# A hybrid attention and linear-attention layer: a gate's bank emptied ahead of the keys' low parts, and one gate half in another bank

## The chip, the core and the metric

The kernel runs on one core of a Trainium2 chip. The metric is the device time of one execution in microseconds, and the time before is the median of three runs. TensorE multiplies matrices into eight PSUM banks; VectorE (DVE) and ScalarE (ACT) read those banks and work on SBUF; GpSimd (POOL) does small jobs on SBUF; transfers are issued from SyncE's queue (SP) for the most part. Each engine takes its instructions in the order in which they stand in its own list and stops at one whose inputs or buffer aren't ready.

## The reference, cut to what matters

One encoder layer on 1024 tokens (a grid of 16 rows of 64) with 16 meta tokens in front, `D_MODEL` = 1024. After an RMS norm one projection gives all parts; eight pairs of heads do neighbourhood attention on the grid, four heads do gated linear attention in both directions. Both are gated with SiLU, joined, projected back and added to the input.

```
z = rmsnorm(h) @ w_in
gq, gk, gv, r_f, r_b, g_gate, nq, nk, nv, n_gate = split(z)
# neighbourhood attention, 16 heads of 64
qn, kn = rmsnorm(nq), rmsnorm(nk)
o_na = softmax(qn kn^T * scale + bias over an 8 x 16 window and 16 meta keys) @ nv * silu(n_gate)
# gated linear attention, 4 heads, both directions, chunked
o_gla = rmsnorm(scan(q, k, v, decay_f) + reversed scan(q, k, v, decay_b)) * silu(g_gate)
out = h + concat(o_gla, o_na) @ w_out
```

Everything is float32 to the caller. The kernel splits each operand of a large product into a high part and a low part (what the high part leaves out), and makes the product from three matmuls: high x high, high x low, low x high.

## The kernel before, in words

**A filler and a main line.** TensorE's list is put together when the program is built. The *filler* is a generator of the large projections, in which there is always something to multiply; the *main line* is the attention of the eight pairs (`attn_all`), and after it the four scans (`gla`). The class `Sched` keeps an estimated TensorE clock, `S.pe`. The main line yields `("gap", ns)` to let the filler issue that much estimated work, `("to", x)` to let it run up to a point, and `("need", key)` to let it run until `key` is in `S.done`. Work that should come some time later is put off with `S.defer(ns, fn)`. So numbers such as `PK_NS`, `TAIL_NS` and `ATTN_NS` set where an instruction stands, on every engine at once; they aren't waits on the chip.

**The projections.** For each pair `p` the filler issues `dense_na(p)`, eight tiles `pn_na` (b = 0 to 7) of queries, keys and values with 8 x 3 matmuls each, and then `dense_gate(p)`, the pair's gate, transposed, in two halves of 512 tokens (`pz_na`, 8 x 3 matmuls each; the second half lags by four steps). These tiles take turns in two PSUM banks, tag `pd`. A bank is free again when VectorE or ScalarE has read it. A gate's half is read by `gate_evac` (L480), one VectorE instruction that multiplies it by the tokens' norm factors and writes it to `ng`. After the last pair come the scans' projections in the same two banks: queries and keys (`gz`, tiles `pz_gz`), values (`gv`), and the scans' gates (`gg`, tiles `pz_gg`, `dense_gg`): two sets of 128 columns, each in two halves of 512 tokens. In the trace's names all four are `pz_gg`, and their evacuations write `gt`.

**The turn of a pair.** When `dense_na(p)` is done, `k_prep(p)` transposes the keys (`kt`) and meta keys (`kmt`) and `q_prep` the first queries (`qt`), while the filler is in the second half of that pair's gate. ScalarE makes the high parts of the keys, `K1` (L667), VectorE the queries' low parts (L699, L701), the meta keys (L670, L671) and then, in four instructions of 64 x 512, the keys' low parts, `K2` (L676). In the trace both K1 and K2 are named `K`. The first scores (`s`, L725 with K1 and L726 with K2) follow some matmuls later. L807 multiplies the previous pair's output, in bank `po`, by its gate.

**A scan.** `gla(h)` first makes the decays (`pdec`, then VectorE's and ScalarE's work on `ga` and `gm`), then goes backward through eight chunks (`state`: a transpose `pk`, its high and low part `kn`, and the three matmuls of `pu`), then forward (`pa`, masked to `at`, in parts `ah`; outputs `po`, which take the bank `po` and a `ps` bank in turn; `post` norms, transposes, `po00t` and so on, and multiplies by the gate, `og`). The gap `PK_NS[h]` stands between the decays and the first transpose `pk`. The filler issues the next projections beside it; weight pieces are split on ScalarE (`wh`, L260) and VectorE (`wl`, L261) as soon as an earlier piece's slot is free.

Of the kernel before, what the change touches and what calls it, by code (L numbers as in the profile page):

```python
# [20 lines left out]
NPAIR = 8  # L21
# [12 lines left out]
ATTN_NS = 7000.0  # L34
NORM_NS = (1500.0, 2100.0)
VLOAD_NS = (1514.0, 651.0)
TAIL_NS = (2000.0, 700.0, 800.0)
PV_AT = (0.5, 0.5, 0.5, 0.6, 0.5, 0.5, 0.5, 0.5)
STEP_AT = (0.78, 2.0, 3.0, 4.0, 4.92, 6.0, 7.08, 8.0)
BWD_NS = (1800.0, 1523.0, 1844.0, 1892.0)  # L40
PK_NS = (2300.0, 2300.0, 2300.0, 2300.0)
AT_NS = 1085.0
R_NS = 2800.0
R0_NS = 1200.0
# [13 lines left out]
LAG = 4  # L58
# [83 lines left out]
def kernel(  # L142
# [28 lines left out]
    S = Sched()  # L171
    ctx.enter_context(tc.manual_schedule())

    def f32(ap):
        return ap.bitcast(F32)
# [13 lines left out]
    def ps_tile(tag, name, bufs):  # L189
        return psum.tile([128, 512], F32, tag=tag, name=name, bufs=bufs)  # L190

    def pt_tile(name, hold):

        S.pt_free = S.pe + hold
        return ps_tile("pt", name, 1)

    def pt_wait():
        if S.pt_free > S.pe:
            yield ("gap", S.pt_free - S.pe)
# [75 lines left out]
    def pump():  # L275
        assert nsplit[0] < allowed[0] or nsplit[0] >= len(pieces)
        piece_split(nsplit[0])
        nsplit[0] += 1

    def release(ns=0.0):  # L280

        allowed[0] += 1
        S.defer(ns, lambda: pump() if nsplit[0] < allowed[0] else None, late=True)
# [17 lines left out]
    def zt_tile(name, pool_=None):  # L301
        if pool_ is not None:
            return pool_.tile([128, 1024], F32, tag="zt2", name=name, bufs=2)
        return shr.tile([128, 1024], F32, tag="zt", name=name, bufs=3)
# [102 lines left out]
    def mm3(ps, ah, al, bh, bl, start, stop):  # L407
        pe.matmul(ps, ah, bh, start=start, stop=False)  # L408
        pe.matmul(ps, ah, bl, start=False, stop=False)  # L409
        pe.matmul(ps, al, bh, start=False, stop=stop)  # L410
# [28 lines left out]
            yield 3 * (c1 - c0) / 2.4  # L439
        return ps  # L440

    def transposed(key, c0, evac, pump_last=False, lag=LAG):

        ps = [None, None]
        ws = slice(c0, c0 + 128)
        order = sorted([(k + lag * half, half, k) for half in range(2) for k in range(NKB)])
        for _, half, k in order:
            if k == 0:
                ps[half] = ps_tile("pd", f"pz_{key[0]}{key[1]}_{c0}_{half}", 2)
            while (key, k) not in split:  # L450
                pump()
            wh, wl, last = split[(key, k)]
            ts = slice(half * 512, half * 512 + 512)
            mm3(ps[half], wh[:, ws], wl[:, ws], uh[:, k, ts], ul[:, k, ts], k == 0, k == NKB - 1)
            if pump_last and half == 1 and last:
                release()
            if k == NKB - 1:
                evac(ps[half], half)
            yield 648
# [16 lines left out]
    def gate_evac(ps, dst, half):  # L476
        hs = slice(512 * half, 512 * half + 512)
        d = seq_view(dst)[:, 4 * half : 4 * half + 4]
        src, r = (t.rearrange("p (b r c) -> p b r c", b=4, r=16, c=8) for t in (ps, rbc[:, hs]))
        dve.tensor_tensor(d, src, r, OP.mult)  # L480
# [148 lines left out]
    def dense_gate(p):  # L629
        g = zt_tile(f"ng{p}")  # L630
        zt[("ng", p)] = g
        yield from transposed(("na", p + 1), 0, lambda ps, half: gate_evac(ps, g, half), pump_last=p == 7)
        silu.append((p, g))
        yield 0


# [2 lines left out]
    def v_load(p):  # L639

        moves = [(VM, vnat[p]), (VM[7::8], vm_scr[p][:, None, :].to_broadcast([16, 8, 128]))]
        return [S.defer(VLOAD_NS[0] + VLOAD_NS[1] * t, lambda m=m: sp.dma_start(*m)) for t, m in enumerate(moves)]

    def k_prep(p):

        kv = kvm[p]
        yield from pt_wait()
        pm = pt_tile(f"kmt{p}", KMT_NS)
        pe.transpose(pm[:, 0:16], kv[:, 0:128], ident[:16, :16])
        dve.tensor_scalar(kmr, pm[:, 0:16], gk_t, None, OP.mult)  # L650
        srcs = []
        for hb in range(2):
            pt = ps_tile("pp", f"kt{p}_{hb}", 2)
            for bb in range(4):
                pe.transpose(pt[:, bb * 128 : bb * 128 + 128], nat[p][4 * hb + bb][:, 128:256], ident)
            srcs.append(pt.rearrange("p (b t) -> p b t", b=4))
        yield ("w", 970)
        yield from pt_wait()
        q_prep(p, 0)
        yield ("w", 220)  # L660
        km = kmr[:, None, :].to_broadcast([128, 8, 16])
        rows = (slice(0, 64), slice(64, 128))
        for hb in range(2):
            bs = slice(4 * hb, 4 * hb + 4)
            for a in range(2):
                r = rows[a]
                act.activation(K1[a][r, bs, 0:128], srcs[hb][r], AF.Copy, scale=gk_t[r])  # L667
        for a in range(2):
            r = rows[a]
            dve.tensor_copy(K1[a][r, :, 128:BLK], km[r])  # L670
            dve.tensor_tensor(K2[a][r, :, 128:BLK], km[r], f32(K1[a][r, :, 128:BLK]), OP.subtract)  # L671
        for hb in range(2):
            bs = slice(4 * hb, 4 * hb + 4)
            for a in range(2):
                r, o = rows[a], rows[1 - a]
                dve.scalar_tensor_tensor(  # L676
                    K2[a][r, bs, 0:128], srcs[hb][r], gk_t[r], f32(K1[a][r, bs, 0:128]), OP.mult, OP.subtract
                )
                pool.tensor_scalar(K1[a][o, bs], f32(K1[a][r, bs]), 1.0, 0.0, OP.mult, OP.add)
# [53 lines left out]
    po = {}  # L733
# [77 lines left out]
    def attn_all():  # L811


        wait, done = [], []

        def turn():
            p, u, *rest = wait.pop(0)
            done.append((p, u, transposes(p, u, *rest)))

        def gather():  # L820
            while done:
                pv(*done.pop(0))

        for p in range(NPAIR + 1):
            if p < NPAIR:
                yield ("need", ("nat", p))
            if wait:
                turn()
                yield ("w", 654)
                yield ("gap", TAIL_NS[0])  # L830
                turn()
                yield ("w", 654)
                yield ("gap", TAIL_NS[1])
            if p < NPAIR:
                yield from k_prep(p)
            if done:
                yield ("gap", TAIL_NS[2])
                gather()
                yield ("w", 1420)
            if p == NPAIR:  # L840
                break
            vload = v_load(p)
            if p in WD_AT:
                wd_load(WD_AT.index(p))
                S.defer(WD_NS, lambda d=WD_AT.index(p): wd_prep(d))
            if p == NPAIR - 2:
                r_static()
            yield ("gap", ATTN_NS - (TAIL_NS[2] + 1420.0 if p else 0.0))
            f0 = S.fill
            f1 = (p + 1) * (NAT_NS + GATE_NS) + (NAT_NS if p < 7 else GLA_NS - 9000.0)  # L850
            for s in range(8):
                if len(wait) == 2:
                    turn()
                    yield ("w", 654)
                wait.append((p, s, *softmax(p, s)))
                yield ("w", 460 if s in (0, 7) else 700)
                if s == 2:
                    wt_load(2 * p + 2)
                a0 = STEP_AT[s - 1] if s else 0.0
                t0, t1 = (f0 + (f1 - f0) * (a0 + (STEP_AT[s] - a0) * x) / 8 for x in (PV_AT[s], 1.0))  # L860
                yield ("to", t0)
                if s in (0, 2, 4):
                    yield from pt_wait()
                    q_prep(p, s // 2 + 1)
                    yield ("w", 220)
                if s % 2 and s > 1:
                    if s == 3:
                        for m in vload:
                            m()
                    gather()  # L870
                    yield ("w", 1420)
                yield ("to", t1)
            wt_load(2 * p + 3)
# [96 lines left out]
    def dense_gg(h, between=None):  # L970
        key = ("gg", h)
        g = gpool[0].tile([128, 2, 1024], F32, tag="gt", name=f"gt{h}")
        for f in range(2):
            if f == 1 and between is not None:
                between()
            evac = lambda ps, half: gate_evac(ps, g[:, f], half)
            yield from transposed(key, 128 * f, evac, pump_last=f == 1)
        gts[h] = g
        S.done.add(("gg", h))
        yield 0  # L980
# [40 lines left out]
    def gla(h):  # L1021
# [105 lines left out]
        act.activation(ma, mg, AF.Exp, scale=-T16, bias=mt[:, 48:49])  # L1127
        yield ("gap", PK_NS[h])

# [345 lines left out]
```

## Time and profile before

| | |
|---|---|
| median of three runs | 1137.01 us (1136.85 to 1138.11) |
| the profiled execution | 1136.87 us, its span 1134.5 us |
| TensorE busy | 1112.4 us, 98% of the span |
| VectorE, ScalarE, GpSimd busy | 731.1, 549.6, 207.9 us |
| mean granted TensorE clock | 0.998 |
| eight pairs of attention, with their projections | about the first 610 us |
| scans and output projection | the rest |

Rows of the timeline read: start in us from the span's start, duration in us, engine, line, operation, output<-inputs, shape, count, and in brackets the idle time before it with what ended it. `PEld` is TensorE's weight load, which runs ahead of the matmul. Matmuls overlap: their starts, not their durations, give their pace. Rows of the view of waits read: who waited, for whom, and then us in total, number of waits, the longest. `+6 lines` has to be kept in mind for the new kernel: from its line 633 on its lines have higher numbers than the old ones (L676 is L681, L807 is L812, L1155 is L1161).

### The profile page before, as it was taken

The numbers are of one execution on the slowest core, as the hardware profiler recorded it, in microseconds if no ns is written. First come the engines' busy times: TensorE is split into PE (matmuls) and PEld (weight loads), VectorE is DVE, ScalarE is ACT, GpSimd is POOL, SyncE is SP. The second block draws the span as 40 slices with busy tenths as digits, with TensorE's granted clock in tenths as the row PEclk, the third lists the DMA queues.
The fourth block names the chain that finished last, engine by engine and source line by source line (L and its number), as shares of the span: only waits on it lengthen the run. The fifth ranks groups of instructions, "written<-read, shape, count | busy, mean of one in ns | idle before, by whom it ended". The sixth has DMA issues, their size and how long they took to land.

```text
span 1134.5 us, 18937 instructions
## 1 busy us (share of the span) xinstructions
PE 1112.4 (98%) x6739; PEld 982.0 (87%) x6739; DVE 731.1 (64%) x1818; ACT 549.6 (48%) x1436; POOL 207.9 (18%) x430
## 2 busy tenths in 40 slices
PE   8999999999999999999999999999999999999998
PEld 8999898988989889898798789889879978888886
DVE  4666666676666767666664875776586577656352
ACT  6756475664656647465555542642443244313120
POOL 2633232332323223232100001001101100000000
PEclk9999999999999999999999999999999999999999
DMA  8810202112021210301124412513512364414132
GB/s 273 234 53 20 103 10 83 55 39 84 9 83 55 79 52 2 119 12 59 50 66 121 141 47 80 154 26 89 166 38 71 107 208 150 121 43 133 50 114 102
DMA packets 75621, 99.20 MB, mean 87 GB/s; under 512 B 6597, under 2 KB 46917, under 8 KB 75529
## 3 DMA queue, kind: packets, MB, share of 16 engines
q1 hardware_dynamic: 69640, 88.70, 25.1%
q0 software_dynamic: 5600, 9.18, 3.1%
q8 instruction: 53, 0.87, 0.3%
q14 instruction: 40, 0.32, 0.1%
q10 hardware_dynamic: 288, 0.14, 0.0%
HBM read 72.76 MB, written 21.04 MB: 83 GB/s over the span
## 4 chain that ended last, share of the span: by engine, by line
PE 81%; DVE 10%; ACT 4%; issue 1%; DMA 1%; POOL 1%; SPq 0%; ACTq 0%; DVEq 0%; POOLq 0%
PE pn_na L408 6%; PE pn_na L409 6%; PE pn_na L410 6%; PE pout L408 5%; PE pout L410 5%; PE pout L409 5%; PE po L797 3%; PE pp L778 3%; PE pn_gv L408 3%; PE pn_gv L409 3%; PE pn_gv L410 3%; PE pz_gz L408 3%; PE pz_gz L409 2%; PE pz_gz L410 2%; PE pz_na L410 2%; PE pz_na L409 2%
## 5 line engine op out<-in xcount | busy, mean ns | idle before, releaser
L408 PE MATMUL pn_na<-wh,uh 128*128 128x384 f32 x512 | 179.0, 350 | 9.0 <-DVE ng L480 7.1
L409 PE MATMUL pn_na<-wl,uh 128*128 128x384 f32 x512 | 173.2, 338 | 0.2 <-DVE wl L261 0.2
L410 PE MATMUL pn_na<-wh,ul 128*128 128x384 f32 x512 | 172.9, 338 | 0.0
L261 DVE SCALAR_TENSOR_TENSOR wl<-raw,gT,wh 128x256 fp32r<-128x256 f32 (+4 forms) x168 | 89.6, 571 | 38.3 <-ACT wh L260 37.3
L408 PEld LDWEIGHTS pn_na<-wh,uh 128*128 128x128 f32 x512 | 96.6, 189 | 16.6 <-DVE ng L480 9.3
L408 PE MATMUL pout<-wh,oh 128*128 128x512 f32 x256 | 103.2, 403 | 0.2 <-DVE acc L1327 0.2
L260 ACT ACTIVATE wh<-raw,gT 128x256 fp32r<-128x256 f32 (+4 forms) x168 | 87.9, 576 | 28.5 <-PE pz_gz L409 18.0
L410 PE MATMUL pout<-wh,oh 128*128 128x512 f32 x256 | 101.4, 396 | 0.0
L409 PE MATMUL pout<-wl,oh 128*128 128x512 f32 x256 | 101.3, 396 | 0.0
L409 PEld LDWEIGHTS pn_na<-wl,uh 128*128 128x128 f32 x512 | 96.9, 189 | 0.9 <-DVE wl L261 0.5
L410 PEld LDWEIGHTS pn_na<-wh,ul 128*128 128x128 f32 x512 | 96.7, 189 | 0.1
L750 ACT ACTIVATE P<-P,sm 128x384 f32<-128x384 f32 x96 | 58.5, 609 | 78.0 <-DVE sm L745 77.3
L1327 DVE TENSOR_TENSOR acc<-acc,pout 128x512 f32<-128x512 f32 x64 | 43.8, 685 | 66.7 <-PE pout L410 66.7
L213 POOL TENSOR_SCALAR post<-post 128x1 f32<-128x1 f32 x32 | 6.7, 209 | 379.4 <-ACT on L1203 379.4
L214 POOL TENSOR_TENSOR ss<-ss,epsm 128x4 f32<-128x4 f32 x64 | 74.7, 1167 | 5.3
L408 PE MATMUL pn_gv<-wh,uh 128*128 128x256 f32 (+1 forms) x256 | 75.1, 293 | 0.0
L745 DVE CUSTOM_DVE_ANT_0 P<-s,wt 128x416 f32<-128x416 f32 (+1 forms) x128 | 65.4, 547 | 12.6 <-PE s L726 11.7
L409 PE MATMUL pn_gv<-wl,uh 128*128 128x256 f32 (+1 forms) x256 | 72.7, 284 | 0.0
L410 PE MATMUL pn_gv<-wh,ul 128*128 128x256 f32 (+1 forms) x256 | 72.7, 284 | 0.0
L766 DVE TENSOR_SCALAR P<-P,sm 128x384 f32<-128x384 f32 (+1 forms) x128 | 58.3, 455 | 11.5 <-ACT P L750 0.5
L410 PEld LDWEIGHTS pout<-wh,oh 128*128 128x128 f32 x256 | 48.2, 188 | 11.7
L408 PEld LDWEIGHTS pout<-wh,oh 128*128 128x128 f32 x256 | 48.2, 188 | 11.6 <-issue 0.7
(345 smaller groups left out, 2803.8 us busy)
## 6 DMA issues: line engine op xcount, KB each, us to landing
raw<-in_w_na_dram SPq DMA_DIRECT2D x56, 256.0 KB, 3.4
v_scr<-gvst SPq DMA_DIRECT2D x64, 128.0 KB, 2.3
raw<-in_w_o_dram SPq DMA_DIRECT2D x32, 256.0 KB, 3.0
oin<-o_scr SPq DMA_DIRECT2D x32, 256.0 KB, 3.0
v<-v_scr POOLq DMA_DIRECT2D x4, 1536.0 KB, 9.4
VM<-vnat SPq DMA_DIRECT2D x8, 512.0 KB, 3.5
o_scr<-ng SPq DMA_DIRECT2D x8, 512.0 KB, 2.8
raw<-in_w_gz_dram SPq DMA_DIRECT2D x16, 256.0 KB, 2.7
```

Source lines behind the costliest of these rows:

```text
L214: pool.tensor_tensor(dst, dst, epsm[: dst.shape[0], :eng_n], OP.pow)
L260: act.activation(wh[:, ts], r[:, ts], AF.Copy, scale=g)
L261: dve.scalar_tensor_tensor(wl[:, ts], r[:, ts], g, f32(wh[:, ts]), OP.mult, OP.subtract)
L408: pe.matmul(ps, ah, bh, start=start, stop=False)
L409: pe.matmul(ps, ah, bl, start=False, stop=False)
L410: pe.matmul(ps, al, bh, start=False, stop=stop)
L745: dve.tensor_tensor_reduce(P[:, :n], ps[:, :n], wt[2 * p + a][:, off : off + n], -1.0, 3.0e38, OP.add, OP.min, mx)
L750: act.activation(loc, loc, AF.Exp, scale=-1.0, bias=mx, accum_out=sm[:, a : a + 1])
L766: dve.tensor_scalar(loc, loc, r, None, OP.mult)
L778: pe.transpose(pp[:w, c * 128 : c * 128 + 128], Ps[a][0][:, c0 : c0 + w], ident)
L797: pe.matmul(po[0][64 * a : 64 * a + 64, u4 * 128 : u4 * 128 + 128], V[:, 64 * a : 64 * a + 64], PT[a][:w, c * 128 : c * 128 + 128], start= ...
L1327: dve.tensor_tensor(a, a, ps, OP.add)
```

## The change

The diff, whole but for its context lines. `transposed` takes the tag of each half's bank as a parameter.

```
-PK_NS = (2300.0, 2300.0, 2300.0, 2300.0)
+PK_NS = (3500.0, 2300.0, 2300.0, 2300.0)
...
-    def transposed(key, c0, evac, pump_last=False, lag=LAG):
+    def transposed(key, c0, evac, pump_last=False, lag=LAG, tags=(("pd", 2), ("pd", 2))):
...
-                ps[half] = ps_tile("pd", f"pz_{key[0]}{key[1]}_{c0}_{half}", 2)
+                ps[half] = ps_tile(tags[half][0], f"pz_{key[0]}{key[1]}_{c0}_{half}", tags[half][1])
...
         silu.append((p, g))                      # dense_gate
+        S.done.add(("gate", p))
...
+    k_at = [0.0]
...
+        k_at[0] = S.pe                           # k_prep, behind the meta keys, ahead of the K2 loop
+        yield ("need", ("gate", p))
         for hb in range(2):
...
-                yield ("gap", TAIL_NS[2])        # attn_all
+                yield ("gap", TAIL_NS[2] - (S.pe - k_at[0] if p < NPAIR else 0.0))
...
-            yield ("gap", ATTN_NS - (TAIL_NS[2] + 1420.0 if p else 0.0))
+            yield ("gap", ATTN_NS - (TAIL_NS[2] + 1420.0 if p else S.pe - k_at[0]))
...
-            yield from transposed(key, 128 * f, evac, pump_last=f == 1)      # dense_gg
+            tags = (("pd", 2), ("pd", 2) if f else ("po", 1))
+            yield from transposed(key, 128 * f, evac, pump_last=f == 1, tags=tags)
```

There are three parts. At the turn of each pair the program waits, while it is built, until the filler has issued the whole gate, and only then issues the four K2 instructions; the gaps behind it are shortened by what the filler issued meanwhile. In `dense_gg` the second half of the first 128 columns takes the bank `po` in place of a `pd` bank. And in scan 0 the gap ahead of the first `pk` is 3500 in place of 2300 estimated ns.

VectorE at the turn from pair 1 to pair 2, first before, then changed (`ng` from `pz_na_0_1` is the evacuation of the gate's second half, `K_0`, `K_1` with `kt` are the K2 parts of the two heads):

```order
L671 TENSOR_TENSOR K_1_94<-kmr,K_1_92 64x8x16
L676 SCALAR_TENSOR_TENSOR K_0_93<-kt_0_1569,gk_t,K_0_91 64x4x128
L676 SCALAR_TENSOR_TENSOR K_1_94<-kt_0_1569,gk_t,K_1_92 64x4x128
L676 SCALAR_TENSOR_TENSOR K_0_93<-kt_1_1574,gk_t,K_0_91 64x4x128
L676 SCALAR_TENSOR_TENSOR K_1_94<-kt_1_1574,gk_t,K_1_92 64x4x128
L480 TENSOR_TENSOR ng_1478<-pz_na_0_1_1513,rbc 128x4x16x8
L807 TENSOR_TENSOR ng_695<-po_1430,ng_695 128x4x16x8
```

```order
L674 TENSOR_TENSOR K_1_94<-kmr,K_1_92 64x8x16
L480 TENSOR_TENSOR ng_1478<-pz_na_0_1_1513,rbc 128x4x16x8
L681 SCALAR_TENSOR_TENSOR K_0_93<-kt_0_1569,gk_t,K_0_91 64x4x128
L681 SCALAR_TENSOR_TENSOR K_1_94<-kt_0_1569,gk_t,K_1_92 64x4x128
L681 SCALAR_TENSOR_TENSOR K_0_93<-kt_1_1574,gk_t,K_0_91 64x4x128
L681 SCALAR_TENSOR_TENSOR K_1_94<-kt_1_1574,gk_t,K_1_92 64x4x128
L812 TENSOR_TENSOR ng_695<-po_1430,ng_695 128x4x16x8
```

The evacuation moved ahead of the four K2 instructions, at this turn and at the seven others; at the last one a weight split `wl` moved with it. TensorE's, ScalarE's, GpSimd's and SyncE's lists are the same through the whole attention.

VectorE in scan 0 from the second columns' first evacuation on, before and changed (`pk` and `pu` are the backward steps, `hm,gm` the forward decay's scan):

```order
L480 TENSOR_TENSOR gt_7351<-pz_gg_128_0_7502,rbc 128x4x16x8
L261 SCALAR_TENSOR_TENSOR wl_7561<-raw_7397,gT,wh_7560 128x256 x2
L1155 TENSOR_TENSOR kn_7572<-pk_7570,kn_7572 128x128
L261 SCALAR_TENSOR_TENSOR wl_7582<-raw_7411,gT,wh_7581 128x256 x2
L1155 TENSOR_TENSOR kn_7594<-pk_7592,kn_7594 128x128
L1178 TENSOR_SCALAR SB_7569<-pu_7597,c_7479 128x256
L1131 SCALAR_TENSOR_TENSOR mt_7432<-mt_7432,gkm_6654 128x16
L1072 SCALAR_TENSOR_TENSOR ga_7488<-hm,gm_7489 128x1024
L480 TENSOR_TENSOR gt_7351<-pz_gg_128_1_7524,rbc 128x4x16x8
```

```order
L480 TENSOR_TENSOR gt_7351<-pz_gg_128_0_7502,rbc 128x4x16x8
L261 SCALAR_TENSOR_TENSOR wl_7561<-raw_7397,gT,wh_7560 128x256 x2
L261 SCALAR_TENSOR_TENSOR wl_7575<-raw_7411,gT,wh_7574 128x256 x2
L1161 TENSOR_TENSOR kn_7586<-pk_7584,kn_7586 128x128
L480 TENSOR_TENSOR gt_7351<-pz_gg_128_1_7524,rbc 128x4x16x8
L261 SCALAR_TENSOR_TENSOR wl_7597<-raw_7426,gT,wh_7596 128x256 x2
L1161 TENSOR_TENSOR kn_7612<-pk_7610,kn_7612 128x128
L1184 TENSOR_SCALAR SB_7583<-pu_7615,c_7479 128x256
L1137 SCALAR_TENSOR_TENSOR mt_7432<-mt_7432,gkm_6654 128x16
L1078 SCALAR_TENSOR_TENSOR ga_7488<-hm,gm_7489 128x1024
```

The first `kn` now has two pairs of weight splits ahead of it, and the last evacuation of the gates stands ahead of the decay's scan.

VectorE at the first forward step of scan 0, before and changed (`gt` times `gq` and `gk` are the four gate products, `og` the gated output):

```order
L1207 SCALAR_TENSOR_TENSOR on_7810<-po_7775,post_7809,gn 128x256
L614 TENSOR_TENSOR gt_7351<-gt_7351,gq_6516 128x512 x2
L614 TENSOR_TENSOR gt_7351<-gt_7351,gk_6517 128x512 x2
L1217 TENSOR_TENSOR og_7845<-po00t,gt_7351 128x256
L1235 TENSOR_TENSOR at_7851<-pa_7848,tri 128x128
L1236 COPY_PREDICATED at_7851<-tri,pa_7848 128x128
L1238 CAST ah_7854<-at_7851 128x128
```

```order
L1213 SCALAR_TENSOR_TENSOR on_7816<-po_7792,post_7815,gn 128x256
L614 TENSOR_TENSOR gt_7351<-gt_7351,gq_6516 128x512
L261 SCALAR_TENSOR_TENSOR wl_7846<-raw_7455,gT,wh_7845 128x256 x2
L614 TENSOR_TENSOR gt_7351<-gt_7351,gq_6516 128x512
L614 TENSOR_TENSOR gt_7351<-gt_7351,gk_6517 128x512 x2
L1223 TENSOR_TENSOR og_7859<-po00t,gt_7351 128x256
L1241 TENSOR_TENSOR at_7865<-pa_7862,tri 128x128
L1242 COPY_PREDICATED at_7865<-tri,pa_7862 128x128
L1244 CAST ah_7868<-at_7865 128x128
```

A weight split now stands between the first two gate products. In scans 1, 2 and 3 all lists keep their order.

## The prediction, made before the changed kernel ran

> **What bounds the kernel now.** I read the page's busy shares first, then TensorE's waits, the timeline around each wait, and last the windows of stretches without one.
>
> ```profile
> span 1134.5 us, 18937 instructions
> PE 1112.4 (98%) x6739; PEld 982.0 (87%) x6739; DVE 731.1 (64%) x1818; ACT 549.6 (48%) x1436; POOL 207.9 (18%) x430
> ```
>
> TensorE is busy for 98% of the span, so a change is worth what it takes from TensorE's pauses, or adds to them. These are the pauses that the change is about, from the view of waits (in total, how many, the longest; the whole list comes to 18 us):
>
> ```profile
> PE pn_na L408 <- DVE ng L480: 7.1, 7, 1.3
> PE pz_gg L408 <- DVE gt L480: 2.6, 2, 1.5
> ...
> PE pz_gz L408 <- DVE ng L480: 1.6, 1, 1.6
> ```
>
> All ten waits name L480, the evacuation of a gate's bank: seven at the turns to pairs 1 to 7, one at the turn to the scans, two inside the scans' gates. One turn in the timeline:
>
> ```profile
> 195.29 0.40 PE L410 MATMUL pz_na<-uh,wl 128*128 128x512 f32 x1
> ...
> 198.81 3.04 DVE L676 SCALAR_TENSOR_TENSOR K<-kt,gk_t,K 64x512 fp32r<-64x512 f32 x4
> ...
> 201.16 0.34 PE L409 MATMUL pn_na<-wl,uh 128*128 128x384 f32 x1
> ...
> 201.33 0.34 PE L410 MATMUL pn_na<-wh,ul 128*128 128x384 f32 x1
> ...
> 201.89 0.69 DVE L480 TENSOR_TENSOR ng<-pz_na,rbc 128x512 f32<-128x512 f32 x1
> ...
> 202.50 0.68 DVE L807 TENSOR_TENSOR ng<-po,ng 128x512 f32<-128x512 f32 x1
> ...
> 202.63 0.44 PE L408 MATMUL pn_na<-wh,uh 128*128 128x384 f32 x1 [0.96 <-DVE ng L480]
> ...
> 202.91 0.34 PE L409 MATMUL pn_na<-wl,uh 128*128 128x384 f32 x1
> ...
> 204.42 0.29 PE L726 MATMUL s<-K,Q 128*128 128x272 f32 x1
> ```
>
> The gate's second half was complete at 195.69. VectorE could have emptied it at 198.81, but first made the four low parts of the keys (3.04 us); the next projection tile but one, `pn_na` of b=1, needs that bank from 201.50 on and gets it at 202.58. A wait costs more than its idle time: matmuls start 0.17 us apart (201.16, 201.33), the next start came 1.30 later, and the one behind it after 0.28. That is (1.30 - 0.17) + (0.28 - 0.17) = 1.24 for a listed 0.96: idle time plus 0.28, of which I take 0.27 for every wait (the 512-wide ones, 0.235 apart, give 0.26).
>
> **The change, part by part.** *The turns.* The second half's evacuation now stands before the four low parts. Its input has been there since 195.69, so it runs from 198.81 to 199.50, and TensorE asks for the bank at 201.50: 2 us to spare. The other turns have the same rows in the same order (the low parts' x32 are 742 to 758 ns each), so all eight waits go: 7.1 + 1.6 + 8 x 0.27 = **10.9 us**. Bounds: the idle time alone is 8.7; by the weight loads' waits it is 9.3 + 2.1 = 11.4:
>
> ```profile
>   PEld pn_na L408: 9.3, 7
> ...
>   PEld pz_gz L408: 2.1, 1
> ```
>
> What is late next: the low parts end 0.69 later, at 202.54, while TensorE comes 1.24 earlier. Their first reader is the second `s` matmul, L726: 204.42 - 1.24 = 203.18, 0.6 us to spare. At the first turn the wait is longer (1.31 + 0.27 = 1.58); the low parts would end at 62.22 + 3.04 + 0.69 = 65.95, the reader come at 67.84 - 1.58 = 66.26, 0.3 us to spare. The turn to the scans is in the last two fences: its wait is 1.65 + 0.27 = 1.92, and there one weight split (0.51) also goes ahead of the low parts; they end at 545.76 + 0.69 + 0.51 = 546.96 at the latest, the reader comes at 549.53 - 1.92 = 547.61.
>
> ```profile
> 62.22 3.04 DVE L676 SCALAR_TENSOR_TENSOR K<-kt,gk_t,K 64x512 fp32r<-64x512 f32 x4
> ```
>
> ```profile
> 66.05 0.44 PE L408 MATMUL pn_na<-wh,uh 128*128 128x384 f32 x1 [1.31 <-DVE ng L480]
> ...
> 67.84 0.29 PE L726 MATMUL s<-K,Q 128*128 128x272 f32 x1
> ```
>
> ```profile
> 545.76 0.69 DVE L480 TENSOR_TENSOR ng<-pz_na,rbc 128x512 f32<-128x512 f32 x1
> 546.37 0.51 DVE L261 SCALAR_TENSOR_TENSOR wl<-raw,gT,wh 128x288 fp32r<-128x288 f32 x1
> ```
>
> ```profile
> 546.50 0.50 PE L408 MATMUL pz_gz<-uh,wh 128*128 128x512 f32 x1 [1.65 <-DVE ng L480]
> ...
> 549.53 0.28 PE L726 MATMUL s<-K,Q 128*128 128x272 f32 x1
> ```
>
> [...] L807 and the store behind it move by under 0.1 us; TensorE needs neither before the next pair's outputs, some 20 us later. Nothing else moves on any engine before the scans, and the reordered pacing gaps leave TensorE's order as it was, so I cost them at nothing.
>
> *The bank of the scans' gates.* The first columns' second half goes to `po`, so the second columns' second half takes the first half's bank, long empty. Two waits, 2.6 + 2 x 0.27 = **3.1 us** (2.6 to 3.7), go: 1.46 + 0.27 = 1.73 of it in scan 0, the other 1.36 in scan 2. `po` is free then: it is used by the attention's and the scans' outputs alone, and a scan's outputs begin only when its gates are done.
>
> *What takes their place.* Behind both waits VectorE works for some 10 us without a pause, and TensorE now comes to that stretch sooner. Scan 0 as it is:
>
> ```profile
> 632.23 0.50 PE L408 MATMUL pz_gg<-uh,wh 128*128 128x512 f32 x1 [1.46 <-DVE gt L480]
> ...
> 634.40 0.91 ACT L260 ACTIVATE wh<-raw,gT 128x256 fp32r<-128x256 f32 x2 [0.54 <-PE pz_gg L409]
> ...
> 634.94 0.88 DVE L261 SCALAR_TENSOR_TENSOR wl<-raw,gT,wh 128x256 fp32r<-128x256 f32 x2 [1.08 <-ACT wh L260]
> ...
> 637.23 0.27 PE L1152 MATMUL pk<-ident,ga 128*128 128x128 f32 x1
> ...
> 639.40 0.29 DVE L1155 TENSOR_TENSOR kn<-pk,kn 128x128 fp32r<-128x128 f32 x1
> ...
> 639.81 0.32 PE L410 MATMUL pu<-v,kn 128*128 128x256 f32 x1
> ```
>
> VectorE's run starts with the weight split, which can move up by ScalarE's 0.54 alone. The later first transpose (`PK_NS`) lets two groups of three matmuls pass, 2 x 0.70: `pk` comes at 637.23 - 1.73 + 1.40 = 636.90, and the last `pu` matmul, three groups behind it as before, at 639.48. The new order has a second pair of splits (0.80) ahead of `kn`, which so ends at 639.69 - 0.54 + 0.80 = 639.95: **+0.5 us** (0 to 0.8).
>
> A second one is in scan 0's forward part:
>
> ```profile
> 663.66 1.29 DVE L614 TENSOR_TENSOR gt<-gt,gk 128x512 f32<-128x512 f32 x2
> ...
> 664.01 0.38 PE L1215 MATMUL po00t<-ident,on 128*128 128x128 f32 x2
> ...
> 664.86 0.42 DVE L1217 TENSOR_TENSOR og<-po00t,gt 128x256 f32<-128x256 f32 x1
> ...
> 665.85 0.23 DVE L1238 CAST ah<-at 128x128 fp32r<-128x128 f32 x1
> ...
> 666.83 0.40 PE L409 MATMUL pz_gz<-ul,wh 128*128 128x512 f32 x1
> ...
> 667.26 0.91 ACT L260 ACTIVATE wh<-raw,gT 128x256 fp32r<-128x256 f32 x2 [3.98 <-PE pz_gz L409]
> 667.30 0.28 PE L408 MATMUL po<-vx,ah 128*128 128x256 f32 x1
> ```
>
> The matmul `po<-ah` comes 3.29 behind the transpose `po00t`. In the new order a weight split stands after the first of the four gate products, and its slot is freed by the matmul group right in front of `po00t`. With P for that transpose: the slot's L409 starts at P - 0.47, ScalarE's half follows 0.43 later and VectorE's split 0.55 after that, at P + 0.51 to 1.39; three products follow (0.64 each, to 3.2), then `og`, and the cast ends 1.22 behind `og`'s start: P + 4.4, against P + 3.3. **+1.2 us** with the restart (0, if the split waits for nothing; 2.2, the split's 0.88 and a 1.3 us pause in front of it, if none of the present margin of 1.2 is left).
>
> ```profile
> 830.76 0.28 DVE L1155 TENSOR_TENSOR kn<-pk,kn 128x128 fp32r<-128x128 f32 x1
> ...
> 831.84 0.28 PE L410 MATMUL pu<-v,kn 128*128 128x256 f32 x1
> ```
>
> In scan 2 the order is unchanged; VectorE gains about the same 0.54 and TensorE 1.36, and the margin of 831.84 - 831.04 = 0.80 covers the difference of 0.82 but for a trace, there and at the `pu` two steps on: **+0.15** (0 to 0.5).
>
> Sum: -10.9 - 3.1 + 0.5 + 1.2 + 0.15 = -12.1. The profiled execution took 1136.87 us (the span and 2.4 around it), 0.14 under the median of 1137.01; 1136.87 - 12.1 = **1124.8 us**.
>
> **The rivals.** *No new waits* (0.20): the run on VectorE keeps up, and all of 14.0 stays: 1122.9. For it: in the present trace neither `kn` nor `ah` is waited for in scan 0; against it: the two sums above miss by 0.5 and 1.1. *The keys' low parts become the wait* (0.10): if they end 1.0 us later than worked out, `s` waits 0.4 with 0.1 for its restart at seven turns and 0.8 at the first, 4.3 in all: 1129.1. It decides where a margin of 0.6 (0.3 at the first turn) is used up. For it: they are moved back, in front of a reader that comes sooner; against it: no row shows work that would delay them further. *The turns' wait stays* (0.04), because the bank is held by something else than the evacuation's place: then only the scans change, -3.1 + 1.85, 1135.6. Against it: the wait ends 0.05 behind L480's end. *Slower* (0.03): with its pauses gone TensorE is granted a lower clock. The price is in the windows (columns: stretch, length, busy time of five engines, clock, DMA):
>
> ```profile
> 0.00:70.00 70.00, 65.47 (x358) 61.58 (x358) 40.10 (x101) 47.35 (x127) 30.00 (x56) 0.98 0.73 224
> ...
> 825.00:925.00 100.00, 100.00 (x608) 87.93 (x607) 67.27 (x157) 40.25 (x90) 7.55 (x18) 1.00 0.34 98
> ```
>
> With the first stretch's 0.98 in the rest too, 70 + (1124.8 - 70)/0.98 = 1146; below 0.989 the gain is gone. But 100 us without a pause ran at 1.00. [...]
>
> **How the numbers follow.** The forecast has 0.63, with 1123.5 to 1126.5 as its own range. From the clean case with 0.6 below it to the late low parts: 1122.3 to 1128.5. A difference of 0.2% (2.3 us) is about what can be told here: the first three cases are faster (0.93, with a little left for a mishap), the fourth is no change (0.04), the fifth slower (0.03).
>
> **What would show it.** Right: no wait of `pn_na` or `pz_gz` on `ng` L480 in the waits, none of `pz_gg` on `gt`; L480's second half directly behind the casts of the meta keys; new waits of `pu` on `kn` near 639 and of `po` on `ah` near 665 (both earlier by some 10 us), under 2 us together. Wrong: `s` waiting for K, the old waits still there, or a clock below 0.99.

## The result

The changed kernel takes 1124.2 us (median; 1123.46 to 1125.54) against 1136.93 for the kernel before, measured beside it on the same chip: a ratio of 0.9885, 95% interval 0.987 to 0.99. It is faster by 1.15%. The profiled execution took 1124.28 us, where 1124.8 was forecast. Its page (span; busy time and share of the span, by engine):

```profile
span 1122.3 us, 18940 instructions
PE 1109.8 (99%) x6739; PEld 981.6 (87%) x6739; DVE 730.5 (65%) x1818; ACT 549.3 (49%) x1436; POOL 207.8 (19%) x430
```

The mean granted clock was 1.000 (0.998 before). TensorE's largest waits in the changed kernel (us in total, how many, the longest):

```profile
PE po L802 <- DVE PT L789: 2.1, 3, 1.0
PE po L408 <- DVE ah L1244: 1.6, 2, 0.9
PE pn_na L408 <- ACT uh L360: 1.1, 1, 1.1
PE warm L345 <- POOL ones L341: 1.0, 1, 1.0
PE pu L410 <- DVE kn L1161: 0.9, 3, 0.3
PE pn_na L408 <- ACT wh L260: 0.6, 1, 0.6
PE pu L408 <- ACT kn L1160: 0.4, 1, 0.4
```

The three rows that the prediction began with, of `pn_na` and `pz_gz` on `ng` and of `pz_gg` on `gt`, are gone. The largest row now, `po` on `PT`, is no new one: before, as L797, it stood in the same list with 2.2, 3, 1.0. (`PT` is the copy out of PSUM of a transposed piece of the softmax's weights; ScalarE makes it for a pair's first head, VectorE for the second, and the attention's `po`, the product with the values, reads both.) The same turn as in the prediction, VectorE and then TensorE:

```profile
195.38 0.69 DVE L480 TENSOR_TENSOR ng<-pz_na,rbc 128x512 f32<-128x512 f32 x1
195.99 3.07 DVE L681 SCALAR_TENSOR_TENSOR K<-kt,gk_t,K 64x512 fp32r<-64x512 f32 x4
199.09 0.69 DVE L812 TENSOR_TENSOR ng<-po,ng 128x512 f32<-128x512 f32 x1
```

```profile
197.90 0.34 PE L410 MATMUL pn_na<-wh,ul 128*128 128x384 f32 x1
198.07 0.34 PE L408 MATMUL pn_na<-wh,uh 128*128 128x384 f32 x1
198.24 0.34 PE L409 MATMUL pn_na<-wl,uh 128*128 128x384 f32 x1
...
199.63 0.29 PE L730 MATMUL s<-K,Q 128*128 128x272 f32 x1
199.75 0.29 PE L731 MATMUL s<-K,Q 128*128 128x272 f32 x1
199.88 0.29 PE L730 MATMUL s<-K,Q 128*128 128x272 f32 x1
200.00 0.29 PE L731 MATMUL s<-K,Q 128*128 128x272 f32 x1
```

The evacuation ends at 196.07. The matmul that waited before is the one at 198.07 (at 202.63 in the fence of the kernel before), and it now starts 0.17 behind the one in front of it. The low parts end at 199.06.

Where the time went can be read matmul by matmul, since TensorE's list has 6739 matmuls in both kernels and the same order outside scan 0: the n-th start of one trace less the n-th start of the other is the time won up to there. The table is worked out from both traces in that way.

| stretch, in us of the kernel before | forecast | measured |
|---|---|---|
| start-up, to 28 | 0 | -0.67 |
| the eight turns, 28 to 550 | -10.9 | -10.90 |
| scans 0 and 1, 550 to 800 | -1.73 + 0.5 + 1.2 = -0.03 | -0.33 |
| scan 2, 800 to 840 | -1.36 + 0.15 = -1.21 | -1.20 |
| the rest | 0 | +0.72 |
| sum | -12.1 | -12.38 |

The start-up owes nothing to the change: all engines' lists are the same in both kernels up to the first turn, and among the traces of this study TensorE comes to the 60th microsecond up to 1.5 us sooner or later, by the waits of `pn_na` on `uh` and `wh` (the high parts of the inputs and of the weights; 1.9 us on `wh` before, 1.1 on `uh` and 0.6 on `wh` changed). The clock of 0.998 before belongs here as well: it was 0.66 from 12 to 17 us, and 1.00 over the rest of the start-up, from 28 to 550 us and from 550 us on. So the gain behind the start-up is not one of the clock.

### The profile page after: what moved, and what is told of

Its sections match the earlier page's. It is cut to its first block, busy times and chain, and to the rows that moved or that the text cites. A ratio compares the mean times of both kernels' runs of the same rounds, so it can differ in the third digit from the quotient of the medians.

```text
span 1122.3 us, 18940 instructions
## 1 busy us (share of the span) xinstructions
PE 1109.8 (99%) x6739; PEld 981.6 (87%) x6739; DVE 730.5 (65%) x1818; ACT 549.3 (49%) x1436; POOL 207.8 (19%) x430
## 4 chain that ended last, share of the span: by engine, by line
PE 87%; DVE 5%; ACT 3%; DMA 2%; issue 1%; POOL 1%; SPq 0%; DVEq 0%; ACTq 0%; POOLq 0%
PE pn_na L408 7%; PE pn_na L410 6%; PE pn_na L409 6%; PE pout L408 5%; PE pout L410 5%; PE pout L409 5%; PE po L802 4%; PE pp L783 3%; PE pn_gv L408 3%; PE pn_gv L410 3%; PE pn_gv L409 3%; PE pz_na L410 3%; PE pz_na L409 3%; PE pz_na L408 3%; PE pz_gz L408 3%; PE pz_gg L408 3%
## 5 line engine op out<-in xcount | busy, mean ns | idle before, releaser
L408 PEld LDWEIGHTS pout<-wh,oh 128*128 128x128 f32 x256 | 48.2, 188 | 12.1 <-issue 0.7
```

## The experiments

### The turns alone, and the bank alone

The first kernel has the new order at the turns and the scans as before. Against the changed kernel:

```
-PK_NS = (3500.0, 2300.0, 2300.0, 2300.0)
+PK_NS = (2300.0, 2300.0, 2300.0, 2300.0)
...
-            tags = (("pd", 2), ("pd", 2) if f else ("po", 1))
+            tags = (("pd", 2), ("pd", 2))
```

> The turns alone: the evacuation of each gate's second half ahead of the four low parts, the scans as before (both halves of the first columns in pd, first gap 2300). By the theory that each turn's wait is the bank held behind the low parts, all eight waits go and nothing takes their place: 1136.9 - 10.9 = 1126.0 us, with the two waits of pz_gg on gt (2.6 us) still listed. By the rival that the gain came from elsewhere (a clock of 1.00 in place of 0.998, or the start of the program, where a transfer's wait differs from run to run), the turns alone bring less than 7 us: 1130 or more.

Measured: 1126.41 us (1125.73 to 1127.55), ratio 0.9901, 0.9888 to 0.9915. In this trace the waits on `ng` are gone, and the scans' stayed:

```profile
PE pz_gg L408 <- DVE gt L480: 2.6, 2, 1.5
```

The n-th starts differ from the kernel before by -0.84 at 28 us, -11.56 at 550 and -11.54 at 925. So the turns are worth 10.7 us by this trace, and no part of that is given back in the scans. The rival's 1130 or more is out.

The second kernel has `po` for the gates' bank and the old order everywhere else. Against the kernel before (with `transposed` taking tags, as in the change):

```
-            yield from transposed(key, 128 * f, evac, pump_last=f == 1)
+            tags = (("pd", 2), ("pd", 2) if f else ("po", 1))
+            yield from transposed(key, 128 * f, evac, pump_last=f == 1, tags=tags)
```

> The bank alone: the second half of the scans' gates' first columns in po, everything else as before, every engine's list in the order of before. By the theory the waits of pz_gg on gt (1.73 and 1.36 us with their restarts) go in scans 0 and 2, but in scan 0 TensorE then comes to the first transpose of the keys about 0.95 us before the decays are ready, and waits 0.3 us more for kn: -3.1 + 1.3 + 0.15 = -1.6, 1135.3 us. By the rival that a freed bank is worth its whole wait: 1133.8. By the rival that VectorE's stretch behind it takes all of it back: 1136.9.

Measured: 1134.97 us (1133.34 to 1135.62), ratio 0.9975, 0.9967 to 0.9984. The two waits of `pz_gg` are gone and the turns' are all there; and there is one that the kernel before doesn't have, of the transpose `pk` in scan 0:

```profile
PE pn_na L408 <- DVE ng L480: 7.1, 7, 1.3
...
PE pz_gz L408 <- DVE ng L480: 1.6, 1, 1.6
...
PE pk L1157 <- ACT wh L260: 0.9, 1, 0.9
```

The view names `wh`, a weight split on ScalarE that ended last (636.37), but `pk` doesn't read it. It transposes `ga`, the decays times the keys, which VectorE ended at 636.30:

```profile
635.08 1.22 DVE L1103 SCALAR_TENSOR_TENSOR ga<-ga,gk 128x1024 f32<-128x1024 f32 x1
636.51 0.30 PE L1157 MATMUL pk<-ident,ga 128*128 128x128 f32 x1 [0.85 <-ACT wh L260]
```

So TensorE came to the transpose before the decays were ready, as the theory had it. By n-th starts the bank won 1.63 us at scan 0's gates, with 0.1 behind it, and lost 1.01 at this `pk`; scan 2 won 1.20. The whole trace is 1.75 us shorter, 0.2 of that in the start-up; the theory had 1.6. The rival of the whole wait, 1133.8, can't be told from this by the time alone; the wait of `pk` speaks against it. The rival of no gain is out by the time. The two parts on their own took 10.97 and 2.41 us off the 1137.38 measured beside them, 13.4 together; the ratio of the whole change makes 13.1 of it. So they add up.

### The longer gap ahead of scan 0's first transpose

```
-PK_NS = (3500.0, 2300.0, 2300.0, 2300.0)
+PK_NS = (2300.0, 2300.0, 2300.0, 2300.0)
```

> The change without its third part: turns and bank as changed, the gap ahead of scan 0's first transpose at 2300, so that the scans' lists stand as before. By the theory the longer gap only trades one wait for others: without it the first transpose waits about 1 us for the decays and kn 0.2, but the waits on kn (0.43) and ah (1.08) of the changed kernel are not there, so 1124.2 - 0.3 = 1123.9 us. By the rival that the gap is needed, 1125.5 or more: the transpose's wait adds to what is there, or a wait for the second columns' evacuation behind the decay's scan comes with it.

Measured: 1124.92 us (1123.64 to 1125.26), ratio 0.9885, 0.9872 to 0.9899: no difference that can be told from the changed kernel. The waits have changed places; this kernel's rows are

```profile
PE pk L1158 <- ACT wh L260: 0.9, 1, 0.9
...
PE pu L410 <- DVE kn L1161: 0.6, 2, 0.4
PE po L408 <- DVE ah L1244: 0.6, 1, 0.6
```

With the gap, scan 0 pays at `pu` (0.43 us, start to start) and at `po` on `ah` (1.10); without it, 1.02 at `pk`, which waits for the decays as in the kernel with the bank alone. By n-th starts scan 0 is 0.36 us shorter without the gap, which is less than these times resolve. The longer gap is no needed part of the change.

### The low parts made twice: how far is the next wait?

The prediction gave the low parts 0.6 us at a turn (0.3 at the first) before the second `s` matmul would wait for them. Here VectorE makes the low parts of the last four blocks a second time (`hb` is the half of the eight blocks), the same numbers, 1.5 us more at each turn:

```
-                dve.scalar_tensor_tensor(K2 ...)
+                for _ in range(1 + hb):
+                    dve.scalar_tensor_tensor(K2 ...)
```

> The changed kernel, with the last two of the four low parts of the keys made twice (the same values again): 2 x 0.76 = 1.5 us more on VectorE at each turn, behind the evacuation. It measures what is left of the margin ahead of s. If the first scores wait for all four low parts, the margin of 0.6 (0.3 at the first turn) is used up and s waits 0.9 with its restart 0.1 at seven turns and 1.3 at the first: 8.3 us, 1132.5. If they wait only for the low parts of the two key blocks that they read (the first two instructions), s waits for nothing: 1124.2 to 1125.5.

Measured: 1129.39 us (1128.33 to 1129.65), ratio 0.9927, 0.9912 to 0.9942. Neither expectation. `s` waits for nothing, yet the time is 5.2 us up, and the trace has it in a row that grew from 2.1, with a small one beside it:

```profile
PE po L803 <- DVE PT L790: 5.0, 8, 1.0
...
PE po L803 <- ACT PT L788: 0.7, 2, 0.3
```

Three of the first row's waits were there before. Seven are new, five in the first row and the two of the second, one behind each of the first seven turns and some 33 us *behind* it. Two questions follow: why did `s` not wait, and why did 1.5 us of VectorE's work come up so late?

For the first one the code has an answer: the first product `s` of a pair has 272 columns, which are key blocks 0 and 1. It needs the low parts of the first half of the blocks alone. To test that, the first half's were made twice, and then three times:

```
+                for _ in range(2 - hb):         # made twice
...
+                for _ in range(3 - 2 * hb):     # made three times
```

> The changed kernel with the low parts of the first four blocks (`hb` 0) made twice instead of those of the last four: again 1.53 us more of VectorE at each of the eight turns, and now ahead of all four blocks. Theory: the first product `s` of a pair covers 272 columns, which are blocks 0 and 1, so it waits for these low parts alone; they end near 130.47 at the turn shown and `s` begins at 132.57, so 2.1 us were free, and 1.5 more leave 0.6. No wait of `s`, the same lateness of VectorE at the copy of PT behind each turn as with the last blocks made twice, and the same time as there, 1128 to 1129.5 us. Rival (the prediction's margin of 0.2 to 0.6 us, from the end of all low parts to the first `s`): `s` waits 0.9 to 1.3 us at each turn, 7 to 10 us in all, and the time is 1132 us or more.

> The changed kernel with the low parts of the first four blocks made three times, 3.06 us more of VectorE at each turn. Theory (2.1 us free ahead of the first `s`): `s` now waits 0.9 to 1.2 us at each turn, 7 to 10 us in all, and what is left of VectorE's lateness (3.06 less the 0.8 that it took up behind the turn before and less the 1.0 that `s` waits, so about 1.2) is waited for once more at the copy of PT some 33 us on: 8 times 1.2 to 1.5. Sum 17 to 21 us, so 1141 to 1145 us. Rival (margin 0.2 to 0.6): `s` waits 2.5 us and more at each turn, over 20 us by itself, and the time is over 1146 us.

Measured: twice 1129.69 us (1128.54 to 1129.9), ratio 0.9926, 0.9909 to 0.9942; three times 1141.67 us (1140.19 to 1143.31), ratio 1.0032, 1.0019 to 1.0045. Made twice, the first half's low parts cost what the last half's did; again `s` doesn't wait, and the two rows of `po` on `PT` read as in the last fence. By n-th starts this kernel loses 4.4 us at these copies, 0.5 to 0.8 behind each of seven turns; its start-up was 1.3 us longer than the changed kernel's. Made three times, `s` waits at all eight turns, and `po` on `PT` as well:

```profile
PE po L803 <- DVE PT L790: 6.2, 8, 1.0
PE s L732 <- DVE K L682: 5.2, 8, 1.0
```

The turn to pair 1 in TensorE's timeline:

```profile
135.62 0.29 PE L731 MATMUL s<-K,Q 128*128 128x272 f32 x1
135.74 0.29 PE L732 MATMUL s<-K,Q 128*128 128x272 f32 x1
135.87 0.29 PE L731 MATMUL s<-K,Q 128*128 128x272 f32 x1
136.72 0.39 PE L732 MATMUL s<-K,Q 128*128 128x272 f32 x1 [0.56 <-DVE K L682]
```

It is the fourth matmul that waits, the second head's product with its low part. At the turn of the result's fences that part ends, in the changed kernel, two instructions (a quarter of 3.07 us each, 0.77) behind 195.99, at 197.53, and the matmul starts at 200.00: 2.47 us are free, and 3.06 more leave a wait of 0.59. The row above, of the turn before, has 0.56; the same matmul of this turn waited 0.55. So the room ahead of `s` is 2.5 us here and not 0.6 (2.2 at the first turn and the last, where `s` waited 0.98 and 0.88). Over all eight turns `s` took 6.5 us more than with the parts made twice, by n-th starts, where 7 to 10 were expected. The whole time is in the theory's range, 1141 to 1145, with some luck: behind the start-up this kernel lost 16.5 us, a little under the sum's 17, and its start-up was 1.1 us longer than the changed kernel's. The rival, over 1146, is out.

For the second question: behind the turn VectorE stays late because most of what it waits for comes late with it. The waits of VectorE in the changed kernel between 134 and 163 us, whole, and its busy time from 137 on (the columns of the second fence: stretch, length, busy time of TensorE, weight loads, VectorE, ScalarE and GpSimd, clock, DMA):

```profile
DVE sm L769 <- POOL sm L757: 4.8, 8, 1.1
DVE ss L514 <- ACT sq L509: 1.1, 1, 1.1
DVE nat L519 <- POOL ss L214: 0.9, 1, 0.9
DVE kvm L529 <- ACT kvt L528: 0.7, 1, 0.7
DVE kvm L535 <- POOL kvs L214: 0.5, 1, 0.5
DVE sm L769 <- ACT P L760: 0.4, 1, 0.4
DVE kvs L531 <- ACT kvt L530: 0.4, 1, 0.4
```

```profile
137.00:163.00 26.00, 26.00 (x178) 24.70 (x178) 17.60 (x54) 18.38 (x57) 8.68 (x22) 1.00 0.05 13
```

VectorE is idle for 8.4 of these 26 us, but each of the waits is for ScalarE or GpSimd, most of them for the answer to VectorE's own work of a moment ago (`sm`: VectorE's row maxima, ScalarE's exponentials and sums, which GpSimd adds up, and back to VectorE). When VectorE starts late, these answers come late as well: the wait at 140.2 us is 1.10 us long in the changed kernel and in the one with the last low parts twice, where it comes 1.28 later. In the kernel with the last low parts twice, VectorE is 2.1 us behind the changed kernel right after the turn, 1.27 at 137 us and still 1.24 at 163; TensorE is 0.53 behind there. The 0.7 us between the two, which the chain carries through 26 us, are what TensorE waits at the next copy of `PT` (0.88 from start to start): no room was left there.

### What makes that copy of PT late

The two larger waits on `PT` stand at 230.7 and 365.8 us, 1.25 and 1.24 us from start to start, in two pairs in which `wd`, the decays' weights, is prepared: ScalarE makes its high part, behind GpSimd's clearing of `wd`, and VectorE two low parts (0.68 and 0.75 us) a little ahead of the copy. The first idea was the low parts, which were moved into VectorE's idle stretch at the next turn:

```
-WD_LOW_NS = 5000.0
+WD_LOW_NS = 36000.0
```

> The changed kernel with the two low parts of `wd` (0.68 and 0.75 us of VectorE) moved from the stretch ahead of the PT copies at 230.7 and 365.8 us to VectorE's idle stretch at the next pair's turn, behind `kmr`. Theory: these 1.43 us are what makes VectorE's copy of PT late there, and the idle stretch at the turn takes them for nothing; the waits `po <- PT` of 1.25 and 1.24 us go, the third (0.45 at 512.9) stays, and the profiled execution is 1124.28 - 1.25 - 1.24 = 1121.8 us, the median about as much below 1124.2. Rival: the turn has no room left behind the banks now emptied ahead of the low parts; `s` or the gates then wait 1.0 to 1.4 us at two turns, and the time is 1123.8 or more.

Measured: 1124.15 us (1123.71 to 1124.31), ratio 0.9879, 0.9864 to 0.9894: no difference, and the theory falls. The two waits are 1.06 us each, 0.19 and 0.18 less. The time lies where the rival put it, but not by the rival's way: neither `s` nor a gate's tile waits at the turns. Where the low parts stood, VectorE now waits:

```profile
226.79 0.08 DVE L750 DVE_READ_ACCUMULATOR2_ANT sm<- 128x1 f32 x1
227.84 0.17 DVE L769 RECIPROCAL sm<-sm 128x1 f32<-128x1 f32 x1 [0.97 <-POOL sm L757]
```

They had filled a wait for `sm` and cost next to nothing. Set against the pair before, the same instructions are first late at ScalarE's high part of `wd`; ScalarE in the changed kernel (`sq`, squares for the norm of queries and keys, which VectorE adds up in `ss`):

```profile
221.73 0.63 ACT L1010 ACTIVATE wd<-wdst 98x512 fp32r<-98x512 f32 x1 [0.88 <-POOL wd L1009]
222.26 0.46 ACT L509 ACTIVATE sq<-pn_na,rs 128x256 f32<-128x256 f32 x1
```

ScalarE stands for 0.88 us until GpSimd has cleared `wd`, with `sq` behind it in its queue. From there on `sq` is 1.52 us later than in the pair before, VectorE's `ss` 0.94 and the copy of `PT` about 1.1. Two kernels put this one ScalarE instruction behind ScalarE's copy of `PT`, in an idle stretch (2.38 us in the changed kernel); one has the low parts moved as well, the other not:

```
+WD_HIGH_NS = 4100.0
...
-        act.activation(w[0:98], st[0:98], AF.Copy)
+        S.defer(WD_HIGH_NS, lambda: act.activation(w[0:98], st[0:98], AF.Copy))
```

> The changed kernel with `wd`'s low parts in the idle stretch of the next turn, as in the run that moved them alone, and its high part (ScalarE, L1010) later too: behind ScalarE's copy of PT at 223.23 us, in an idle stretch of 2.4 us, instead of ahead of `sq` at 221.73. Theory: there ScalarE waits 0.88 us for GpSimd's clearing of `wd` and then works 0.63 on it, with `sq` queued behind, so `sq` comes 1.52 us late against the pair before, VectorE's `ss` 0.94, and the copy of PT some 7 us on about 1.1. Without it the waits `po <- PT` at 230.7 and 365.8 (1.25 and 1.24 us in the changed kernel, 1.06 with the low parts moved alone) are under 0.2 us; the profiled execution comes 2.1 to 2.5 us under 1124.28, near 1121.9 us, less or more by what the start-up happens to take. Rival: the copy is late through the `kvm` and `kvs` steps or the softmax of these pairs itself; the waits stay at 1.0 us or more and the time at 1123.9.

> The changed kernel with `wd`'s high part alone moved behind ScalarE's copy of PT; the two low parts stay where they were, in VectorE's wait for `sm`. Theory: the high part is the cause by itself, the low parts add at most the 0.19 us a time that moving them gave; the waits `po <- PT` at 230.7 and 365.8 come to 0.2 us or less, and the time is within 0.5 us of the other run's, near 1122.2 us. Rival: both parts are needed (each hides behind the other); the waits stay over 0.8 us and the time over 1123.5 us.

Measured: with both moved 1122.74 us (1121.53 to 1123.08), ratio 0.9865, 0.9848 to 0.9881; with the high part alone 1122.75 (1122.56 to 1123.05), ratio 0.9869, 0.9854 to 0.9884. ScalarE in the second one:

```profile
221.58 0.46 ACT L510 ACTIVATE sq<-pn_na,rs 128x256 f32<-128x256 f32 x1
...
222.92 0.64 ACT L1011 ACTIVATE wd<-wdst 98x512 fp32r<-98x512 f32 x1
```

and what is left of the wait in either kernel's list of TensorE's waits (2.1 in the changed kernel):

```profile
PE po L803 <- DVE PT L790: 0.2, 1, 0.2
```

By n-th starts the kernel with both moved has won 1.06 + 1.04 us at the two copies against the changed kernel, and with the high part alone moved 0.87 + 0.86, which leaves 0.38 at each from start to start: the theory had 0.2 there. With the 0.19 and 0.18 of the low parts alone, the two moves add up. The profiled executions took 1123.08 and 1123.05, since their start-ups were 1.28 and 0.78 us longer than the changed kernel's. The medians are 1.5 us under the changed kernel's 1124.2; the intervals of the ratios overlap (0.9848 to 0.9881, 0.987 to 0.99), so the time alone makes the gain likely, and the vanished waits show where it comes from. The rivals, waits of 1.0 and of 0.8 us or more, are out.

## Why the prediction was right, and where it wasn't

**The turns, -10.9.** Right in size and mechanism: -10.90 by n-th starts in the changed kernel, -10.7 with the turns alone. The term for the restart, 0.27 on top of each listed wait, held: at a listed idle time of 0.96 the first matmul alone came 1.13 us sooner, the one behind it 0.1 more. The rival in which the turns' wait stays, at 1135.6, is out.

**The low parts behind the evacuation.** Their ends were forecast well: 0.69 us ahead of the second `s` matmul at the turn shown (199.06 against 199.75; 0.64 forecast), 0.38 at the first (0.31 forecast). But the step that called this the room up to the next wait was wrong. It set the end of all four low parts against the first reader of the first two. The room ahead of `s` is 2.5 us, and what runs out first is another one, the copy of `PT` 33 us on, which the prediction didn't look at. The price named for late low parts, 4.3 us for 1.0 of lateness through `s`, was thus no forecast of anything: 1.5 us cost 5.2 to 5.5 by the medians (some 4.4 of it at the copies), and not through `s`. The forecast held all the same: in the changed kernel `s` waits for nothing, and the copies of `PT` cost what they did before. (The whole range's upper end, 1128.5, was also to reach this case, which the prediction itself put at 1129.1.)

Evacuation and first low part overlap: 195.99 is 0.61 behind 195.38, and the evacuation takes 0.69. So do L480 and L807 at the same turn of the kernel before, where 202.50 is 0.61 behind 201.89 and L480 takes 0.69. The forecast ends of the low parts were added up without these 0.08 us.

**The scans' bank, -3.1.** Right: 1.63 at the matmul that waited and 0.1 behind it in scan 0 (1.73 forecast), and 1.36 in scan 2 (1.36 forecast).

**The new waits, +1.85.** All are there, at their places; in scan 0 they cost 1.47 by n-th starts, with 1.7 forecast. `pu` on `kn`, forecast +0.5:

```profile
626.41 1.66 DVE L261 SCALAR_TENSOR_TENSOR wl<-raw,gT,wh 128x256 fp32r<-128x256 f32 x4
627.99 0.28 DVE L1161 TENSOR_TENSOR kn<-pk,kn 128x128 fp32r<-128x128 f32 x1
```

```profile
627.78 0.27 PE L409 MATMUL pu<-v,kn 128*128 128x256 f32 x1
628.33 0.39 PE L410 MATMUL pu<-v,kn 128*128 128x256 f32 x1 [0.28 <-DVE kn L1161]
```

Two pairs of splits ahead of `kn`, and a start 0.55 behind the one before, 0.43 more than the usual distance. And `po` on `ah`, forecast +1.2:

```profile
655.56 0.39 PE L410 MATMUL pz_gz<-uh,wl 128*128 128x512 f32 x1
656.89 0.38 PE L408 MATMUL po<-vx,ah 128*128 128x256 f32 x1 [0.94 <-DVE ah L1244]
```

which is 1.10 more than the usual distance. The way there is the forecast one too: the transpose `po00t` starts at 652.51, the split 0.50 behind it and the cast's end 4.32 (0.51 and 4.4 forecast). Scan 2's +0.15 came as well, in waits too short for the list. At the third `pu` matmul the weight load starts 0.05 us behind the end of `kn`, at 818.55 and two steps on at 823.78, and TensorE loses 0.07 and 0.10 there; so -1.36 became -1.20. The rival without new waits, 1122.9, is out by these rows. That the forecast's 1124.8 came so near to the 1124.28 of the profiled execution is luck in one respect: what it left out, -0.67 in the start-up and +0.72 behind scan 2, cancels. Of the latter 0.34 is the wait of `po` on `ah` in scan 3, which was there before (0.54 from start to start, now 0.88, and 0.68 to 0.97 in the nine further kernels), and most of the rest stands near the end of the output projection. Why those two differ was not followed up.

**The clock.** TensorE ran at 1.000 with its pauses gone, so the slower case, 1146, is out.

**The longer gap**, which the forecast carried as part of scan 0's two sums, was not judged on its own; the run without it shows that it moves the wait and is worth nothing that can be measured.

## What to carry to other kernels

Where a bank's evacuation has its input long before the work in front of it in the queue, put it ahead, and price the gain at the listed idle time plus the restart (0.27 us a wait here). Work out the room that the pushed-back work has from each piece's own reader, and follow the pushed-back engine on to the *next* place where the busiest engine waits for it: an engine that is a third idle (VectorE is busy for 65% of the span here) may have no slack at all, if its idle time is spent on answers to its own work. An instruction that must wait for another engine (0.88 us here, for GpSimd's clearing) costs what is queued behind it (`sq`, 1.52 us late, 0.63 of it the instruction's own work), so put it where its queue has nothing to do. And check the name that a view gives to what ended a wait against what the waiting instruction reads.

## What wasn't expected

VectorE's lateness lasted: of 2.1 us behind a turn (0.53 of it TensorE's own) 1.27 were left 5 us later, and 1.24 still 26 us on, although VectorE is busy for only 17.6 of those 26 us. And the two instructions that stood nearest to the late copy, 1.43 us of VectorE's time, were worth 0.19 us each time, while one ScalarE instruction 9 us ahead of it, whose own work is 0.63 us, was worth 0.87.
